# A first mixer fed with a turned copy of x, both first convolutions ahead of the query and key work, and output rows placed among scores and turns

## The chip, the cores and the metric

The kernel runs on one core of a Trainium2 chip. The metric is the time of one execution on the device in microseconds: the median of several runs. A core has TensorE (PE in the rows; weight loads are PEld), VectorE (DVE), ScalarE (ACT), GpSimd (POOL) and the sync engine (SP), each with a queue of its own that it works off in order, and 16 DMA engines. All data are float32.

## The reference

Two transformer blocks over 256 tokens of width 1024, with 16 meta tokens in front in the first. A block is a mixer and a mixture of experts (32 experts, two per token, and a shared one). The change touches the first mixer and the kernel's last lines. The first mixer, cut:

```
h = concat([meta, x]);  z = rms_norm(h, pre_mix_norm) @ w_in
c_q, c_kv, k_pe, gate_b, gate_c, x_in = split(z)          # 256, 128, 32, 3 x 512 columns
q  = (rms_norm(c_q, q_norm) @ w_uq)   -> 8 heads, 64 plain + 32 rope columns
kv = (rms_norm(c_kv, kv_norm) @ w_ukv) -> k_nope, v;  k_rope = rope(k_pe)
attn = causal softmax attention over meta and tokens
u = gate_c * x_in;  y[t] = sum_k conv_w[k] * u[t-2+k];  conv = gate_b * y
out = concat([rms_norm(attn), rms_norm(conv)]) @ w_out
h = h + rms_norm(out);  h = h + rms_norm(moe(rms_norm(h)))
```

The second block is alike, with differential attention and retention as its mixer, and a final norm.

## The kernel before

**Products.** Every large product of the mixers is done as three: each operand is split into a high half and the rest (a low half), and `mm3` (L319 to L321) adds high by high, high by low and low by high into one PSUM bank. Of a weight the high half is a ScalarE copy (L294) and the low half a subtraction (L295) on VectorE for a chunk's first half and on GpSimd for its second. `prepare` makes one such part; `part` hands out the oldest prepared one and prepares the next. The first mixer has 20 parts: 12 for the three convolution inputs (four each) and 8 for the output weights, of which the conv branch's four come first.

**Weights.** Chunks of 1 MB stream through 26 slots. `plan` gives their order; the sync engine issues the next load when a slot is free (`ahead`, `fits`). An engine's work is in the order in which the program writes it; nothing reorders it later.

**The first mixer's sequence.** x and the meta tokens are loaded row by row of tokens and turned on TensorE: 24 transposes (L432, L434). ScalarE and VectorE take the eight turned pieces out as high and low halves times the norm's gain. W_a (the columns for c_q, c_kv and k_pe) is split into four parts (`split_wa`), and z comes out in three banks (eight steps of k). Squares of x give the row scales, positions give angles, and ScalarE's Sin gives the rope factors. Then: `conv(0)` (gate_c, four quarters m of 24 matmuls), transposes of c, query product (L606) and key/value products, `conv(1)` (x_in, taps in `gated`), `turn_q` (16 transposes, L649), `conv(2)` (gate_b, ends in `conv_done`, which leaves the conv branch's mixed parts `mc` in halves). Scores (L679, mask L681) follow: four banks of two heads for the first 128 queries, eight banks of one head for the second; VectorE takes the maximum (L682), ScalarE the exponential (L685), then four multiplications by the reciprocal sums (L692), two on VectorE and two on GpSimd. `w_out` adds one part i of the four of a branch into a bank for a half t of the queries and a half e of the columns. Parts 0 and 1 of `mc` come first (24 matmuls), then all 24 turns of the probabilities (`turn_p`, L727), the branch's row scale (`feat_rstd`, `turn_m`), parts 2 and 3 for t = 0, `attend(0)`, those for t = 1, and `attend(1)`. `attend` (L742, L747) leaves the attention branch's halves `ma`, whose rows with the last four weight parts follow, then the residual, the router and MoE 1, whose first expert product is L1501.

**The tail.** The last norm of the output multiplies by its gain in quarters as MoE 2 ends (`after`, L1184), sums squares, and scales by the root (L1202, L1204) before the stores.

Of the kernel before, what the change touches and what calls it, by code (L numbers as in the profile page):

```python
# [75 lines left out]
def layout(i):  # L76
# [5 lines left out]
    o["pos"] = np.ascontiguousarray(f["positions"].reshape(2, 128).T)  # L82
    kt = lambda w: w.reshape(-1, 128, w.shape[1]).transpose(1, 0, 2)
    w = g("w_in")
# [46 lines left out]
    for n, grp in enumerate(CONST_GROUPS):  # L131
        o[f"c{n}"] = np.concatenate([cs[k] for k in grp], 1)
    o["c2"] = np.concatenate([o["c2"], o.pop("lam")], 1)
# [18 lines left out]
def plan():  # L152
# [14 lines left out]
    yield from (("wa", 0), ("wa", 1), ("wc", 0), ("wc", 1), ("wuq",), ("wukv",), *[("wc", j) for j in range(2, 6)])  # L167
# [16 lines left out]
class Builder:  # L184
# [73 lines left out]
    def source(self, key):  # L258
        if key[0] == "pmg":
            r = self.a["pmg"]  # L260
            return [bass.AP(tensor=r.tensor, offset=r.offset, ap=[[0, 128], [1, D]]), self.a["wr"][0]]
        if key == ("dn2", 15, 3):
# [82 lines left out]
    def setup(self):  # L345
        nc, P, a = self.nc, self.P, self.a
        self.h = P.tile([128, 2, D], F32, name="h")
        nc.sync.dma_start(self.h[:, 0], a["x"][0:128])
        self.meta = self.slot([NM, D], "meta")
        nc.sync.dma_start(self.meta, a["meta"])  # L350
        nc.sync.dma_start(self.h[:, 1], a["x"][128:256])
        self.k = self.const(P.tile([128, self.coff[0][1]], F32, name="const0"), 0, nc.scalar)
        self.small = P.tile([128, self.sn], F32, name="small")
        nc.scalar.dma_start(self.small, a["small"])
        self.pos = P.tile([128, 2], I32, name="pos")
        nc.scalar.dma_start(self.pos, a["pos"])
        self.s = {k: self.small[:, o:o + w] for k, (o, w) in self.soff.items()}
        self.bef = P.tile([128, 128], BF, name="bef")
        self.onesb = P.tile([128, 128], BF, name="onesb")
# [4 lines left out]
        nc.gpsimd.memset(self.mhalf, -0.5)  # L364

    def late_setup(self, before):
# [3 lines left out]
        nc.gpsimd.memset(self.onesb, 1.0)  # L370
# [29 lines left out]
    def mixer1(self):  # L400
# [5 lines left out]
        k1 = self.const(gen, 1, nc.scalar)  # L406
# [17 lines left out]
        piece = lambda i: xp[i // 7][:, i % 7] if i < 14 else self.GS[:, (i - 14) * 258:(i - 14) * 258 + 258]  # L424
        xh, xl = [piece(2 * k) for k in range(8)], [piece(2 * k + 1) for k in range(8)]
        xm = cT[:, 0:128].rearrange("p (k t) -> p k t", t=NM)
        self.ahead()
        self.late_setup(k1["before"])
        ps = [bank() for _ in range(8)]
        for t in range(2):  # L430
            for k in range(8):
                PE.transpose(ps[k][:, NM + t * 128:NM + t * 128 + 128], h[:, t, k * 128:k * 128 + 128], id_)  # L432
                if t == 0:
                    PE.transpose(ps[k][:, 0:NM], meta[:, k * 128:k * 128 + 128], id_[:NM, :NM])  # L434
        wat, wa = [], []

        def split_wa(j):
            raw = self.chunk("wa", j)
            wat.append(raw)
            for e in range(2):  # L440
                w = self.slot([128, 2, 1024], "wa", F32R)
                x = raw[:, e * 832:e * 832 + 832]
                A.activation(w[:, 0, :832], x, AF.Copy)
                (V, nc.gpsimd)[e].tensor_tensor(w[:, 1, :832], x, w[:, 0, :832].bitcast(F32), op=OP.subtract)
                wa.append(w)

        for k in range(8):
            gain, p = s["pmn"][:, k:k + 1], ps.pop(0)
            A.activation(xh[k], p[:, NM - 2:TA], AF.Copy, scale=gain)
            V.scalar_tensor_tensor(xl[k], p[:, NM - 2:TA], gain, xh[k].bitcast(F32), op0=OP.mult, op1=OP.subtract)  # L450
            V.tensor_scalar(xm[:, k], p[:, 0:NM], gain, None, op0=OP.mult)
            if k == 1:
                split_wa(0)
        split_wa(1)
        za = [bank() for _ in range(3)]
        for k in range(8):
# [6 lines left out]
            if k % 4 == 3:  # L463
                self.free(wat[k // 4], *wa[k // 2 - 1:k // 2 + 1])
        idb, tri = sub([128, 64]).bitcast(BF), sub([128, 64]).bitcast(BF)
# [6 lines left out]
        for j, x in ((0, h[:, 0]), (2, meta)):  # L472
            n = x.shape[0]
            for e in range(2):
                A.activation(bank()[:n], x[:, e * 512:e * 512 + 512], AF.Square,
                             accum_out=ss[:n, 3 * e + j:3 * e + j + 1])
        ang = sub([128, 2, 3, 16])
# [21 lines left out]
        for e in range(2):  # L499
            sl = slice(e * 512, e * 512 + 512)  # L500
            V.scalar_tensor_tensor(junk, h[:, 1, sl], 1.0, h[:, 1, sl], op0=OP.mult, op1=OP.mult,
                                   accum_out=ss[:, 3 * e + 1:3 * e + 2])
        V.tensor_tensor(ss[:, 0:3], ss[:, 0:3], ss[:, 3:6], op=OP.add)
        rx = self.rms(ss[:, 0:3], 3, D)
# [6 lines left out]
        p = bank()  # L511
        self.spread(p[:, 0:NM], rx[:NM, 2:3], NM)
        for t in range(2):
            self.spread(p[:, NM + t * 128:NM + t * 128 + 128], rx[:, t:t + 1])
        rxx = sub([128, 258])
        A.activation(rxx, p[:, NM - 2:TA], AF.Square)
# [42 lines left out]
        def conv(i, done):  # L559
            for m in range(4):  # L560
# [213 lines left out]
        for t in range(2):  # L774
# [6 lines left out]
            if t == 0:  # L781
                self.prepare()
# [955 lines left out]
```

## Time and profile before

| | before |
|---|---|
| median of three runs | 936.5 us (935.39 to 937.39) |
| profiled execution | 936.15 us |
| its span, first to last instruction | 934.4 us |
| mean granted TensorE clock | 0.956 of full |
| TensorE / VectorE / ScalarE / GpSimd busy | 845.6 / 389.6 / 227.0 / 118.8 us |
| moved by DMA | 340.88 MB |
| first convolution begins, third ends | 30.24 us, 81.76 us |
| second attend ends | 116.00 us |
| MoE 1's first expert product begins | 143.51 us |

Shares are of the span. Busy time includes waits for data inside an instruction, so a TensorE that is 91% busy is not one at its peak. The trace lets one look at a stretch, an engine or a line alone; the rows used are shown below.

### The profile page before, as it was taken

Reading aid. Unit: us, or ns where it says so; the run is one execution under the profiler, and the core shown is the slowest. Engines: PE = TensorE matmul, PEld = TensorE weight load, DVE = VectorE, ACT = ScalarE, POOL = GpSimd, SP = SyncE. Lnnn points to the kernel's source line nnn. Section 1 sums busy time; section 2 is a strip of 40 time slices with the busy share of each in tenths; the row PEclk is TensorE's granted clock in tenths of the full one; section 3 lists DMA queues with packets and bytes.
Section 4 is the critical chain, followed back from the end, with each engine's and each line's share of the span. In section 5 each row is a group of like instructions: output and inputs, shape, how many; then the busy total and the mean of one; then the engine's idle time right before and its main releaser. Section 6 shows DMA issues by size and latency. Waiting matters only on the chain. (4 is left out here: it accounts for less than half of the span.)

```text
span 934.4 us, 12196 instructions
## 1 busy us (share of the span) xinstructions
PE 845.6 (91%) x4789; PEld 469.0 (50%) x4789; DVE 389.6 (42%) x789; ACT 227.0 (24%) x473; POOL 118.8 (13%) x83
## 2 busy tenths in 40 slices
PE   7999999997967858997989999999999998799995
PEld 4788775553431316996874443434343432334332
DVE  4867672443322368576451224232333331133313
ACT  5346522211110135372312102111111110011113
POOL 3322520000000047634300000000000000000002
PEclk9999999998977897997999999999999999899998
DMA  9925498999999999553799999999999999999994
GB/s 363 415 95 221 160 385 354 420 419 418 420 420 420 421 421 421 219 178 138 271 364 368 421 415 391 421 421 422 420 422 420 421 422 421 416 422 421 421 420 169
DMA packets 48631, 340.88 MB, mean 365 GB/s; under 512 B 5536, under 2 KB 6176, under 8 KB 8112
## 3 DMA queue, kind: packets, MB, share of 16 engines
q1 hardware_dynamic: 47408, 338.55, 88.7%
q10 hardware_dynamic: 1152, 1.41, 0.5%
q8 instruction: 42, 0.69, 0.3%
q14 instruction: 29, 0.24, 0.1%
HBM read 338.88 MB, written 1.05 MB: 364 GB/s over the span
## 5 line engine op out<-in xcount | busy, mean ns | idle before, releaser
L1501 PE MATMUL bank<-chunk,xe 128*64 128x512 f32 (+1 forms) x1536 | 293.6, 618 | 27.8 <-DMA chunk<-in_gu_dram 15.0
L1501 PEld LDWEIGHTS bank<-chunk,xe 128*64 128x64 f32 (+1 forms) x1536 | 88.0, 130 | 218.2 <-issue 197.6
L1574 PE MATMUL bank<-chunk,hids 128*64 128x512 f32 (+1 forms) x736 | 143.3, 618 | 19.9 <-DMA chunk<-in_dn_dram 19.4
L1574 PEld LDWEIGHTS bank<-chunk,hids 128*64 128x64 f32 (+1 forms) x736 | 40.8, 128 | 117.4 <-issue 75.5
L295 POOL TENSOR_TENSOR w<-chunk,w 128x1024 fp32r<-128x1024 f32 x28 | 69.7, 2497 | 78.2 <-ACT w L294 65.4
L1578 DVE SCALAR_TENSOR_TENSOR ys<-bank,wc,ys 128x512 fp32r<-128x512 f32 x46 | 34.5, 750 | 98.1 <-ACT ys L1577 98.1
L1507 DVE TENSOR_TENSOR hids<-bank,hids 128x512 f32<-128x512 f32 x12 | 8.3, 692 | 158.0 <-PE bank L1501 158.0
L1577 ACT ACTIVATE ys<-bank,wc 128x512 fp32r<-128x512 f32 x46 | 31.6, 687 | 143.8 <-PE bank L1574 135.3
L1184 POOL TENSOR_TENSOR out<-acc,rows 128x256 f32<-128x256 f32 x6 | 4.3, 730 | 439.2 <-DVE acc L1692 439.1
L294 ACT ACTIVATE w<-chunk 128x1024 fp32r<-128x1024 f32 x52 | 52.4, 1053 | 22.0 <-DVE w L295 11.5
L1596 DVE TENSOR_TENSOR acc<-acc,bank 128x512 f32<-128x512 f32 x84 | 52.1, 680 | 13.3 <-PE bank L1589 13.3
L1512 DVE SCALAR_TENSOR_TENSOR hids<-bank,misc,hids 128x256 f32<-128x256 f32 (+1 forms) x12 | 6.9, 572 | 113.9 <-ACT hids L1511 70.7
L1506 ACT ACTIVATE hids<-bank 128x512 f32<-128x512 f32 x12 | 7.2, 597 | 181.6 <-PE bank L1501 181.6
L1347 PEld LDWEIGHTS bank<-GS,h 128*128 128x128 f32 x384 | 45.5, 197 | 10.7 <-issue 5.1
L1589 PE MATMUL bank<-ys,GS 128*128 128x512 f32 x184 | 49.5, 408 | 1.3 <-ACT ys L1577 1.3
L1347 PE MATMUL bank<-GS,h 128*128 128x128 f32 x384 | 47.8, 284 | 1.6 <-DVE GS L1355 1.6
L1511 ACT ACTIVATE hids<-bank,misc 128x256 f32<-128x256 f32 (+1 forms) x12 | 6.5, 546 | 136.0 <-PE bank L1501 136.0
L295 DVE TENSOR_TENSOR w<-chunk,w 128x1024 fp32r<-128x1024 f32 x24 | 35.7, 1494 | 8.8 <-ACT w L294 8.7
L948 PE MATMUL bank<-w,xT 128*128 128x512 f32 x144 | 37.8, 422 | 0.6 <-DVE xT L902 0.6
L1589 PEld LDWEIGHTS bank<-ys,GS 128*128 128x128 f32 x184 | 32.5, 188 | 10.9 <-ACT ys L1577 2.2
L948 PEld LDWEIGHTS bank<-w,xT 128*128 128x128 f32 x144 | 29.0, 205 | 7.8 <-DVE xT L902 1.7
L860 POOL TENSOR_TENSOR xn<-h,rows 128x1024 f32<-128x1024 f32 x2 | 4.7, 2388 | 188.3 <-DVE misc L1557 188.3
(401 smaller groups left out, 1187.1 us busy)
## 6 DMA issues: line engine op xcount, KB each, us to landing
chunk<-in_gu_dram SPq DMA_DIRECT2D x192, 1024.0 KB, 19.8
chunk<-in_dn_dram SPq DMA_DIRECT2D x95, 1024.0 KB, 19.8
chunk<-in_wi_dram SPq DMA_DIRECT2D x12, 1024.0 KB, 19.5
chunk<-in_wo_dram SPq DMA_DIRECT2D x8, 1024.0 KB, 15.9
chunk<-in_wc_dram SPq DMA_DIRECT2D x6, 1024.0 KB, 13.6
chunk<-in_sgu_dram SPq DMA_DIRECT2D x2, 1024.0 KB, 9.5
chunk<-in_wa_dram SPq DMA_DIRECT2D x2, 832.0 KB, 6.9
h<-in_x_dram SPq DMA_DIRECT2D x2, 512.0 KB, 5.4
```

Source lines behind the costliest of these rows:

```text
L294: self.nc.scalar.activation(w[:, 0], raw, AF.Copy)
L295: (eng or (self.nc.vector, self.nc.gpsimd)[e]).tensor_tensor(w[:, 1], raw, w[:, 0].bitcast(F32), op=OP.subtract)
L948: PE.matmul(p[t], xT[x][:, 2 * i + k, t * 128:t * 128 + 128], w[:, s, k * 512:k * 512 + 512], start=i + x + s + k == 0, stop=i + x == 4 an ...
L1347: b.nc.tensor.matmul(self.pb[k // 4][:, k % 4 * 128:k % 4 * 128 + 128], b.h[:, t, k * 128:k * 128 + 128], G[:, t].bitcast(F32), start=t == ...
L1501: PE.matmul(g[i][e * C:e * C + C], xe[:, k, e * C:e * C + C], c[:, e, i * 512:i * 512 + 512], start=k == 0, stop=k == 7)
L1506: A.activation(hid, g[0], AF.Silu)
L1507: V.tensor_tensor(hid, g[1], hid, op=OP.mult)
L1574: PE.matmul(y[e * C:e * C + C], hT[:, o:o + C], c[:, f, e], start=q + f == 0, stop=fpc * q + f == FC - 1)
L1577: A.activation(ys[:, 0, i], y, AF.Copy, scale=wc)
L1578: V.scalar_tensor_tensor(ys[:, 1, i], y, wc, ys[:, 0, i].bitcast(F32), op0=OP.mult, op1=OP.subtract)
L1589: PE.matmul(ps[t], S[:, t * 128:t * 128 + 128], ys[:, i, e], start=i == 0, stop=i == 1)
L1596: V.tensor_tensor(o, b.h[:, t, sl] if new else o, p, op=OP.add)
```

## The change

- **Start.** A turned copy of x (1 MB) and of the meta tokens is read from DRAM, and the transposes are gone. The constants, the small vectors and the positions arrive in one transfer; ScalarE does an early copy. TensorE does 60 small bfloat16 products (`warm`) ahead of z. x itself is loaded whole behind W_a. The splits of W_a stand between the pieces k. The squares and the row scale come ahead of the angles.
- **Order of the convolutions.** `conv(0)` and `conv(1)` both stand ahead of the query and key work, and the plan loads all four of their chunks first. `turn_q` goes between the second and third quarter of `conv(2)`.
- **Output rows.** The eight rows of parts 0 and 1 follow one by one the eight scores of the second queries; part 2 follows them, and part 3 stands between the turns. The two attends follow each other. The last two of the attention branch's weight parts, of which one was made by the second call of `part` and one between the attends, are made by `part` behind the second attend.
- **Tail.** The last quarter's gain is multiplied together with the root, and the scaling is 512 columns on ScalarE and twice 256 on VectorE.

The core of the diff:

```diff
-        ps = [bank() for _ in range(8)]
-        for t in range(2):
-            for k in range(8):
-                PE.transpose(ps[k][:, NM + t * 128:NM + t * 128 + 128], h[:, t, k * 128:k * 128 + 128], id_)
...
+        xt = self.slot([128, 8, T], "xt")
+        for j in range(2):
+            nc.sync.dma_start(xt[:, 4 * j:4 * j + 4].rearrange("p k t -> p (k t)"), self.a["xt"][j])
+            raw[j] = self.chunk("wa", j)
+        nc.sync.dma_start(h, self.a["x"].rearrange("(t p) d -> p t d", p=128))
...
         for k in range(8):
-            gain, p = s["pmn"][:, k:k + 1], ps.pop(0)
-            A.activation(xh[k], p[:, NM - 2:TA], AF.Copy, scale=gain)
+            gain = s["pmn"][:, k:k + 1]
+            A.activation(xh[k][:, 2:258], xt[:, k], AF.Copy, scale=gain)
...
+            if k in (1, 3, 4):
+                split_wa(k // 4, k // 3 % 2 if k < 4 else 0)
...
-        conv(0, lambda m, p: V.tensor_tensor(u[:, m], p, rxx, op=OP.mult))
+        conv(0, lambda m, p: V.tensor_tensor(u[:, m], p, rxx, op=OP.mult),
+             between={0: spread_rx})
...
+        conv(1, gated)
...
-        conv(2, conv_done)
+        conv(2, conv_done, {2: turn_q})
...
+        pc = {(t, e): bank() for t in range(2) for e in range(2)}
+        w = [self.part(0) for _ in range(2)]
+        rows = [(t, e, i) for i in range(2) for t in range(2) for e in range(2)]
...
+                if t:
+                    r = rows[h0]
+                    w_out(pc, mc, *r, w[r[2]])
...
+        turn_p(0, 0)
+        turn_p(0, 1)
         for e in range(2):
-            turn_p(0, e)
-            turn_p(1, e)
...
+            w_out(pc, mc, 0, e, 3, w[1])
+        turn_p(1, 0)
+        for e in range(2):
+            w_out(pc, mc, 1, e, 3, w[1])
+        turn_p(1, 1)
...
-        w = [self.part(), self.part()]
-        for t in range(2):
-            for i in range(2):
-                for e in range(2):
-                    w_out(pc, mc, t, e, 2 + i, w[i])
+        for t in range(2):
             for e in range(2):
                 A.activation(mix[:, t, e * 512:e * 512 + 512], pc[t, e], AF.Copy, scale=rc[:, t:t + 1])
             attend(t)
-            if t == 0:
-                self.prepare()
         self.phase(0, 7)
         w = [self.part() for _ in range(4)]
...
             for t in range(2):
+                A.activation(o[:, t, 0:512], o[:, t, 0:512], AF.Copy, scale=r[:, t:t + 1])
+                V.scalar_tensor_tensor(o[:, t, 768:D], moe.acc[:, t, 768:D], r[:, t:t + 1], made["rows"][:, 768:D],
+                                       op0=OP.mult, op1=OP.mult)
+                V.tensor_scalar(o[:, t, 512:768], o[:, t, 512:768], r[:, t:t + 1], None, op0=OP.mult)
```

Three places show the new order. The first is TensorE at the turns of the probabilities, before (w are weight parts, mc the conv branch's mixed parts, P the probabilities, pT and cT turned copies):

```order
L319 MATMUL bank<-w,mc 128x512
L320 MATMUL bank<-w,mc 128x512
L321 MATMUL bank<-w,mc 128x512
L727 MATMUL bank<-const_74,P 128x128 x24
L708 MATMUL bank<-ones,chunk 128x1 x2
L735 MATMUL bank<-const_74,cT 128x128 x2
L319 MATMUL bank<-w,mc 128x512
L320 MATMUL bank<-w,mc 128x512
```
and in the change:

```order
L324 MATMUL bank<-w,mc 128x512
L325 MATMUL bank<-w,mc 128x512
L326 MATMUL bank<-w,mc 128x512
L760 MATMUL bank<-const_72,P 128x128 x8
L324 MATMUL bank<-w,mc 128x512
L325 MATMUL bank<-w,mc 128x512
L326 MATMUL bank<-w,mc 128x512
L324 MATMUL bank<-w,mc 128x512
L325 MATMUL bank<-w,mc 128x512
L326 MATMUL bank<-w,mc 128x512
L760 MATMUL bank<-const_72,P 128x128 x8
```
The 24 turns stood in one piece behind the rows of parts 0 and 1; now rows of part 3 (the six behind the first eight turns, and six more later) stand between them.

The second place is ScalarE from the last weight copies of the softmax's end to the residual, before (L294 is a weight's high half, L313 and L749 an attend's copy and square):

```order
L294 ACTIVATE w<-chunk 128x1024 x2
L779 ACTIVATE mix<-bank,rs 128x512 x2
L313 ACTIVATE ma<-cT 128x4x128
L749 ACTIVATE vy<-bank 128x4x128
L294 ACTIVATE w<-chunk 128x1024
L779 ACTIVATE mix<-bank,rs 128x512 x2
L313 ACTIVATE ma<-cT 128x4x128
L749 ACTIVATE vy<-bank 128x4x128
L375 ACTIVATE bank,nss<-mix 128x512 x2
```
and in the change (L299, L318 and L782 are the same lines):

```order
L810 ACTIVATE mix<-bank,rs 128x512 x2
L318 ACTIVATE ma<-cT 128x4x128
L782 ACTIVATE vy<-bank 128x4x128
L810 ACTIVATE mix<-bank,rs 128x512 x2
L318 ACTIVATE ma<-cT 128x4x128
L782 ACTIVATE vy<-bank 128x4x128
L299 ACTIVATE w<-chunk 128x1024 x2
L385 ACTIVATE bank,nss<-mix 128x512 x2
```
The weight copy between the attends is gone, and two stand behind the second attend's square.

The third is GpSimd around the softmax's multiplications, before (L692 is the multiplication, L295 a low half, L331 a root):

```order
L295 TENSOR_TENSOR w<-chunk,w 128x1024 x6
L692 TENSOR_TENSOR P<-P,gen_87 128x576
L692 TENSOR_TENSOR P<-P,gen_87 128x1088
L295 TENSOR_TENSOR w<-chunk,w 128x1024
L331 TENSOR_TENSOR rs<-ms,mhalf 128x2
L295 TENSOR_TENSOR w<-chunk,w 128x1024 x2
L331 TENSOR_TENSOR rs<-ms,mhalf 128x2
```
and in the change (L730, L300, L336):

```order
L300 TENSOR_TENSOR w<-chunk,w 128x1024 x6
L730 TENSOR_TENSOR P<-P,gen_143 128x576
L730 TENSOR_TENSOR P<-P,gen_143 128x1088
L300 TENSOR_TENSOR w<-chunk,w 128x1024 x2
L336 TENSOR_TENSOR rs<-ms,mhalf 128x2
L300 TENSOR_TENSOR w<-chunk,w 128x1024
L336 TENSOR_TENSOR rs<-ms,mhalf 128x2
```
Behind the multiplications two low halves follow each other where one stood, and one instead of two comes between the roots.

## Rows read from the trace of the kernel before

**Rows 1.** Table of stretches: start:end, length, busy us (instructions) per engine, clock, DMA share, GB/s.

```profile
46.00:70.00 24.00, 24.00 (x141) 19.41 (x140) 14.91 (x24) 9.91 (x17) 4.72 (x2) 0.93 0.29 103
...
150.00:350.00 200.00, 163.36 (x1116) 73.58 (x1108) 71.13 (x140) 35.98 (x82) 12.01 (x8) 0.91 1.01 420
...
450.00:900.00 450.00, 433.17 (x2179) 199.66 (x2179) 140.45 (x297) 68.15 (x130) 5.60 (x5) 0.99 0.99 407
```

**Rows 2.** Timeline of the sync engine's queue: start, length, line, operation.

```profile
144.63 6.33 SPq L255 DMA_DIRECT2D chunk<-in_gu_dram  x8
```

**Rows 3.** Timeline of TensorE, the first expert product of MoE 1.

```profile
143.51 1.92 PE L1501 MATMUL bank<-chunk,xe 128*32 128x512 f32 x16
```

**Rows 4.** Waits of TensorE up to 150 us: line waited for, total, times, longest.

```profile
PE bank L606 <- DVE cT L588: 2.1, 1, 2.1
...
PE bank L679 <- ACT P L685: 1.7, 1, 1.7
```

**Rows 5.** Timeline of TensorE from the scores to the second attend and behind it.

```profile
81.76 0.41 PE L679 MATMUL bank<-kT,qT 96*128 96x144 f32 x2
...
88.76 0.73 PE L679 MATMUL bank<-kT,qT 96*128 96x272 f32 x2 [1.74 <-ACT P L685]
...
90.94 1.24 PE L679 MATMUL bank<-kT,qT 96*128 96x272 f32 x2
...
94.61 0.39 PE L319 MATMUL bank<-w,mc 128*128 128x512 f32 x1
...
98.69 2.78 PE L727 MATMUL bank<-const,P 128*128 128x128 f32 x24
...
116.00 0.50 PE L319 MATMUL bank<-w,ma 128*128 128x512 f32 x1
...
118.88 0.75 PE L708 MATMUL bank<-ones,chunk 128*128 128x1 f32 x4
```

**Rows 6.** Timeline of ScalarE at the start: Sin, and weight copies behind it.

```profile
25.56 0.28 ACT L506 ACTIVATE gen<-gen 128x96 f32<-128x96 f32 x1 [3.16 <-DVE gen L498]
...
25.75 1.99 ACT L294 ACTIVATE w<-chunk 128x1024 fp32r<-128x1024 f32 x2
```

**Rows 7.** Timeline of VectorE: three small operations, and a weight's low half.

```profile
34.31 4.70 DVE L535 TENSOR_TENSOR rs<-rs 128x2 f32<-128x2 f32 x3 [0.82 <-POOL rs L331]
...
41.52 1.22 DVE L295 TENSOR_TENSOR w<-chunk,w 128x1024 fp32r<-128x1024 f32 x1
```

**Rows 8.** Timeline of TensorE: first convolution's first matmul, and what follows its last.

```profile
30.24 0.37 PE L319 MATMUL bank<-xp,w 128*128 128x258 f32 x1
...
41.96 0.23 PE L576 MATMUL bank<-const,cn 16*128 16x16 f32 x1
```

**Rows 9.** Timeline of GpSimd beside rows 7.

```profile
34.24 4.75 POOL L295 TENSOR_TENSOR w<-chunk,w 128x1024 fp32r<-128x1024 f32 x2
```

**Rows 10.** Timeline of VectorE: last maximum, a low half, last reduction of squares.

```profile
92.32 0.44 DVE L682 TENSOR_REDUCE gen<-bank 128x1 f32<-128x272 f32 x1 [0.85 <-PE bank L681]
...
97.18 2.40 DVE L295 TENSOR_TENSOR w<-chunk,w 128x1024 fp32r<-128x1024 f32 x1
...
118.12 1.06 DVE L703 TENSOR_REDUCE chunk<-vy 128x128 f32<-128x512 f32 x1
```

**Rows 11.** Timeline of GpSimd: softmax multiplication, two low halves.

```profile
95.38 1.16 POOL L692 TENSOR_TENSOR P<-P,gen 128x576 f32<-128x576 f32 x1 [12.06 <-DVE gen L691]
...
98.46 3.35 POOL L295 TENSOR_TENSOR w<-chunk,w 128x1024 fp32r<-128x1024 f32 x1
...
112.17 2.36 POOL L295 TENSOR_TENSOR w<-chunk,w 128x1024 fp32r<-128x1024 f32 x1 [6.40 <-ACT w L294]
```

**Rows 12.** Timeline of ScalarE: a weight copy between the attends, last square.

```profile
111.04 1.05 ACT L294 ACTIVATE w<-chunk 128x1024 fp32r<-128x1024 f32 x1
...
117.39 0.58 ACT L749 ACTIVATE vy<-bank 128x512 f32<-128x512 f32 x1
```

**Rows 13.** Timeline of VectorE in the tail.

```profile
926.79 0.75 DVE L1184 TENSOR_TENSOR out<-acc,rows 128x256 f32<-128x256 f32 x2
...
927.46 0.15 DVE L1195 TENSOR_REDUCE nr<-nss 128x1 f32<-128x4 f32 x1
```

More of the change, by code (lines that the diff above doesn't have):

```diff
@@ L165, in experts @@
         yield from ((f"dn{n}", units - 1, j) for j in range(4))
-    yield from (("wa", 0), ("wa", 1), ("wc", 0), ("wc", 1), ("wuq",), ("wukv",), *[("wc", j) for j in range(2, 6)])
+    yield from (("wa", 0), ("wa", 1), *[("wc", j) for j in range(4)], ("wuq",), ("wukv",), ("wc", 4), ("wc", 5))
     yield from (("wo", 2), ("wo", 3), ("wo", 0), ("wo", 1), ("pmg",), ("sgu", 0), ("sgu", 1))
@@ L261, in source @@
             return [bass.AP(tensor=r.tensor, offset=r.offset, ap=[[0, 128], [1, D]]), self.a["wr"][0]]
+        if key[0] == "wa":
+            return [self.a["wa"][key[1]][:, e * 832:e * 832 + 832] for e in range(2)]
         if key == ("dn2", 15, 3):
@@ L364, in setup, with warm @@
         nc.gpsimd.memset(self.mhalf, -0.5)
+        nc.scalar.activation(self.ones[:, 1:2], self.mhalf[:, 0:1], AF.Copy)
+        self.warm(60)
+    def warm(self, n):
+        p = self.bank()
+        for _ in range(n):
+            self.nc.tensor.matmul(p[:, 0:128], self.onesb, self.onesb, start=True, stop=True)
     def late_setup(self, before):
@@ L557, in mixer1, with conv @@
              sin[:, :, None, :].to_broadcast([128, 3, 2, 16]), 3)
-        def conv(i, done):
+        def conv(i, done, then=(), between=()):
             for m in range(4):
+                if m in then:
+                    then[m]()
                 w = self.part()
@@ L752, in mixer1 @@
         self.phase(0, 5)
-        pc = {(t, e): bank() for t in range(2) for e in range(2)}
-        for i in range(2):
-            w = self.part(0)
-            for t in range(2):
-                for e in range(2):
-                    w_out(pc, mc, t, e, i, w)
-            self.free(w)
+        w = [self.part(0), self.part(0)]
+        for t in range(2):
+            for e in range(2):
+                w_out(pc, mc, t, e, 2, w[0])
         for t in range(2):
@@ L763, in mixer1 @@
         self.phase(0, 6)
+        turn_p(0, 0)
+        turn_p(0, 1)
         for e in range(2):
-            turn_p(0, e)
-            turn_p(1, e)
-        self.free(*PP)
+            w_out(pc, mc, 0, e, 3, w[1])
+        turn_p(1, 0)
+        for e in range(2):
+            w_out(pc, mc, 1, e, 3, w[1])
+        turn_p(1, 1)
+        self.free(*PP, *w, mc)
         rc = feat_rstd(rx[:, 0:2])
@@ L1183, in after @@
                                           accum_out=ss[:, t, q:q + 1])
[L1184 to L1187 removed]
+                if q < 3:
+                    self.nc.gpsimd.tensor_tensor(made["out"][:, t, sl], moe.acc[:, t, sl], made["rows"][:, sl],
+                                                 op=OP.mult)
+        self.link = moe, made, ss, r
         return after
```

154 lines of the change are left out of this document (75 added, 79 removed).

## The prediction

> **What bounds the kernel now.** I read the table of stretches first. From 150 us on, except in the second mixer, the DMA engines are never free: 420 GB/s and a busy share of 1.01 from 150 to 350, 407 GB/s and 0.99 from 450 to 900 [rows 1]. The first mixer lies ahead of those stretches, so the next question is what lets that stream begin. The sync engine's queue shows it: a burst of eight expert chunks is issued from 144.63 [rows 2], right after TensorE begins the first expert product at 143.51 [rows 3]. The slots that the burst fills are freed by that product. Behind it the stream runs at its own pace, so **a microsecond that the first mixer ends earlier or later moves the end of the kernel by a microsecond**. From 46 to 70 DMA stands at 0.29: bandwidth is not what the first mixer waits for. The list of waits says that TensorE hardly waits there either, 2.1 us for the normalised c_q (L606) and 1.7 us for a bank among the scores (L679) [rows 4]. So TensorE's sequence, with its clock, is the path up to 143.51, and every new wait on it is paid in full.
>
> Half clock follows both waits. From 90.94 the pair of score matmuls takes 1.24 us where the one at 88.76 took 0.73, and the output rows come back to their pitch at 94.61 [rows 5]: 3.67 us go to work that takes 2.1 at the pitches on either side, so 1.6 us are lost. After the wait of 2.1 the table shows 24 us at a mean clock of 0.93 [rows 1], which is 1.7 us lost. I use **1.6 us for one spell at half clock**.
>
> The sum is made against the profiled execution's 936.15 us; the median of the runs shown, 936.5, lies 0.35 above, well inside the 0.2% (1.9 us) that a measurement of this kernel can tell from no change.
>
> **The change, part by part.** Below, S is the end of the third convolution and start of the scores, L the end of the last score, T the end of the second attend.
>
> *Start, -1.4.* The 24 transposes leave TensorE, and the 60 warm-up products stand where it has nothing to do, since it waits for the turned copy. But the first convolution doesn't wait for TensorE alone. Its second weight half is copied by ScalarE right behind the Sin, at 25.75 now [rows 6], and the Sin stays behind the angles on VectorE, with the squares of x now ahead of them. I estimate Sin at 25, the copy until 26.2 and the low half, 1.22 us [rows 7], until 27.5. Three quarters of a convolution, at 2.9 each from 30.24 to 41.96 for four [rows 8], then end at 36.3, 5.6 us before the old 41.96. Most of that goes back: the second convolution now follows at once, and its first weights have their low half on VectorE, behind c's normalisation, the rope and the first u. Those stand behind GpSimd's low halves: three small VectorE operations took 4.70 us [rows 7] while GpSimd made two of them in 4.75 us [rows 9], and now three stand in a row. By these rows the low half comes at about 39.9: 3.6 us. Half a spell at half clock or a slightly longer wait on c_q takes 0.6. S is 1.4 earlier. Bounds: nothing given back, -5.6; all given back, 0. I stand nearer the second because every step of the giving back has a row. The extra megabyte at the start moves later transfers by about 2.5 us at 420 GB/s [rows 1]; the cover is the weights' lead, and without it the copy above starts that much later, which the bound of 0 holds.
>
> Those rows show small VectorE operations standing for as long as GpSimd's subtractions run. The Trainium skill, SBUF — State Buffer, section "SBUF: two separate sides", says that VectorE and GpSimd share one port pair as an exclusive lock, and whichever began second blocks entirely. It speaks against this change, which puts more of GpSimd's long subtractions in a row. The trace agrees: 4.70 beside 4.75. Were it not so, the start would keep about 4 us more; that case is the third rival.
>
> *Scores, -0.3.* Output rows of the first two mixed parts move between the scores of the second half of the queries. The wait for a bank remains: the first exponentials free the banks as late as before (7.0 us after S, at 88.76 [rows 5]). From there six scores at 0.57 and six rows of three matmuls at 0.23 [rows 5] take 7.6, with 0.4 for the exponentials that free the following banks, and a half-clock spell 1.6 as now: rows done 16.6 after S, where now it is 16.9, from 81.76 to 98.69 [rows 5]. But **the last score, L, comes only 0.7 us before the last row**, no longer six.
>
> *First new wait, +4.7.* What was cover is gone. Before, the last maximum is taken at 92.32 [rows 10], GpSimd starts its two softmax multiplications at 95.38 and the low half of the fourth weight part at 98.46, 3.35 us long [rows 11]: it is there at 101.81, 9.5 after the last score, while TensorE has eight output rows, 24 turns and four more rows to do. In the changed sequence TensorE does after L one row (0.7), four rows of the third part (2.8), four turns, then waits for GpSimd's first multiplication (L + 4.2) and does four more turns; at L + 4.7 it wants that low half, which still stands third in GpSimd's queue: L + 9.4. Queued behind the waiting matmul are all remaining turns and both attends, and nothing on TensorE can go round it. Bounds: 3.7 if the low half takes the 2.36 of row 112.17 [rows 11] instead of 3.35, 4.9 by the rows as they stand. VectorE has again a low half beside it, as at 97.18 [rows 10], so I take the upper part.
>
> *Between, 0.* The work from 98.69 to 116.00 [rows 5] is the same matmuls in another order. The turned q and the spread of the row scales, moved inside convolutions, last as long there as where they stood.
>
> *Second new wait, +4.2.* The last two parts of the output weights are now prepared after the second attend; one of them was done between the attends on ScalarE at 111.04 (1.05 us) [rows 12] and GpSimd at 112.17 (2.36) [rows 11]. Now both copies stand in ScalarE's queue behind the last square, which ends at 117.97 [rows 12], 2.0 after T = 116.00 [rows 5]: copies done at T + 3.0 and T + 4.0, the third part's low half on VectorE behind the reduction that ends at 119.18 [rows 10], so T + 4.4, the fourth's on GpSimd at T + 6.4. TensorE needs them from T + 1.4. The group of twelve matmuls that ended at T + 2.9 (118.88 [rows 5]) ends at T + 7.1. Bounds: 3.6 if ScalarE's copies overlap the square, 4.5 if GpSimd's runs beside a VectorE operation.
>
> *Clock, +2.4.* Both known waits of 1.7 to 2.1 us were followed by a spell at half clock. The first new one is longer than either and of one piece: 1.6. The second comes in three pieces with matmuls between: half, 0.8. Bounds 0 and 3.2 for both.
>
> *End, -0.3.* The last quarter's multiplication (two of 0.75 together on VectorE at 926.79) no longer stands ahead of the sums at 927.46 [rows 13]; the squares on ScalarE limit the gain to about 0.3. Bounds 0 and -0.7.
>
> Sum: -1.4 - 0.3 + 4.7 + 4.2 + 2.4 - 0.3 = +9.3, so **945.5 us**.
>
> **The rivals.** *Both splits in time (faster).* If the fourth weight part's low half were ready within 4.7 us after the last score, and the last two weight parts before T + 1.4, neither wait would exist: -1.4 - 0.3 - 0.3 gives 934.1, and without the spell among the scores, which the rows between them could prevent, 932.5. It decides at GpSimd: three of its instructions, 3.1 + 3.35 us after reciprocals that need the last maximum, must take less than 4.7 in all. For it: the multiplications would be shorter with VectorE idle. Against: each stands on TensorE's path by its own queue, and even 2.36 for the third leaves 8.4. Chance 0.18.
>
> *Only one wait bites.* Second alone: 936.15 - 2.0 + 4.2 + 0.8 = 939.2; first alone: 936.15 - 2.0 + 4.7 + 1.6 = 940.5. For it: the two waits are independent, and either needs only one GpSimd run to end some 4 us sooner than its row says. Chance 0.13.
>
> *The start keeps its gain.* If the lock on the low halves doesn't hold c back, S comes up to 5.6 earlier; with both waits that is 945.5 - 4.2 = 941.3. For it: TensorE has 6.5 us less to do there. Against: rows 7 and 9. Chance 0.08.
>
> *The warm-up doesn't do what it says:* the products end, TensorE stands for the copies of x, and z runs slowly as now. TensorE is not what the first convolution's second quarter waits for, so this changes no sum and is inside the first term.
>
> **How the numbers follow.** The forecast, both waits with at least one spell, has 0.61. Its own range is the bounds: below, no spells (-2.4), the shorter low half (-1.0) and half the start's giving back (-2.1), not all at once, 940.5; above, the full clock price (+0.8), S unmoved (+1.4), waits at their upper ends (+0.5) and a little for later transfers, 949.5. The single-wait cases reach to 938. I range 937.5 to 949.5, which leaves out the first rival. Faster by over 0.2%: most of the first rival, 0.16. Within 0.2%: its rest, where a small wait eats the gain, and the lower end of the single-wait case, 0.07. Slower: 0.77.
>
> **What would show it.** Right: TensorE's list of waits gains a row for the low half of a weight part made by GpSimd, some 4 to 5 us, in the middle of the turns, and rows for the last two parts, 3 to 4 us in all, after the second attend; the first expert product begins near 153, and the burst of eight expert chunks a microsecond later. Wrong: these rows are missing or under a microsecond, the second convolution runs on from the first without a wait, or that product begins later without the end moving, which would break the first step.

## The result, and the profile after

The change makes the kernel slower: 949.89 us median (949.03 to 952.37), against 936.18 (935.39 to 937.39) for the kernel before in the same comparison. The ratio is 1.015, with a 95% interval of 1.0128 to 1.0172. The forecast was 945.5 with a range of 937.5 to 949.5: the direction and the two waits were right, the size was 4.4 us short, and the time lies 0.4 us outside the range.

The profiled execution took 949.79 us, its span is 948.0, 13.6 more than before. TensorE's waits up to the first expert product, in the view whose columns are line waited for, total, times and longest, are these:

```profile
PE bank L325 <- POOL w L300: 5.6, 2, 4.3
PE bank L326 <- DVE w L300: 4.3, 2, 3.5
PE bank L645 <- DVE cT L627: 2.1, 1, 2.1
PE bank L324 <- ACT w L299: 1.9, 2, 1.3
...
PE bank L714 <- ACT P L720: 1.3, 1, 1.3
...
PE bank L325 <- DVE w L300: 0.9, 1, 0.9
```

Where [rows 4] have two waits, there are now also four rows for weight parts (`w`), made by GpSimd, VectorE and ScalarE; some of their waits stand in the first two convolutions, the others in the turns and behind the second attend. The timeline of TensorE answers to [rows 3, 5]:

```profile
42.07 0.39 PE L326 MATMUL bank<-xp,w 128*128 128x258 f32 x1 [3.52 <-DVE w L300]
...
83.22 0.41 PE L714 MATMUL bank<-kT,qT 96*128 96x144 f32 x2
...
90.06 0.72 PE L714 MATMUL bank<-kT,qT 96*128 96x272 f32 x2 [1.25 <-ACT P L720]
...
97.28 0.22 PE L716 MATMUL bank<-gen 128*128 128x128 bf16 x1
...
98.08 0.39 PE L324 MATMUL bank<-w,mc 128*128 128x512 f32 x1
...
102.21 0.48 PE L324 MATMUL bank<-w,mc 128*128 128x512 f32 x1
107.03 0.79 PE L325 MATMUL bank<-w,mc 128*128 128x512 f32 x1 [4.34 <-POOL w L300]
...
122.67 0.50 PE L324 MATMUL bank<-w,ma 128*128 128x512 f32 x1
...
125.64 0.49 PE L324 MATMUL bank<-w,ma 128*128 128x512 f32 x1 [1.31 <-ACT w L299]
127.03 0.50 PE L325 MATMUL bank<-w,ma 128*128 128x512 f32 x1 [0.89 <-DVE w L300]
...
129.25 0.79 PE L325 MATMUL bank<-w,ma 128*128 128x512 f32 x1 [1.26 <-POOL w L300]
...
130.26 0.85 PE L746 MATMUL bank<-ones,chunk 128*128 128x1 f32 x4
...
156.68 1.91 PE L1530 MATMUL bank<-chunk,xe 128*32 128x512 f32 x14
```

The scores begin at 83.22 instead of 81.76; the eight rows are done at 98.08, 14.9 later instead of 16.9; the wait of 4.34 stands in the turns; the second attend ends at 122.67 instead of 116.00; behind it the group of twelve matmuls takes 7.6 instead of 2.9; and the first expert product begins at 156.68 instead of 143.51. From there to the end it is 791.3 us against 790.9. So 13.2 of the 13.6 us arise ahead of that product, and the step "a microsecond there is a microsecond at the end" held. The other engines, in the same timeline:

```profile
25.62 0.28 ACT L523 ACTIVATE gen<-gen 128x96 f32<-128x96 f32 x1 [2.29 <-DVE gen L521]
...
32.83 7.07 POOL L300 TENSOR_TENSOR w<-chunk,w 128x1024 fp32r<-128x1024 f32 x3
...
32.90 4.70 DVE L554 TENSOR_TENSOR rs<-rs 128x2 f32<-128x2 f32 x3 [0.82 <-POOL rs L336]
...
40.80 1.22 DVE L300 TENSOR_TENSOR w<-chunk,w 128x1024 fp32r<-128x1024 f32 x1
...
100.59 3.11 POOL L730 TENSOR_TENSOR P<-P,gen 128x576 f32<-128x576 f32 x2 [15.98 <-DVE gen L729]
103.66 5.65 POOL L300 TENSOR_TENSOR w<-chunk,w 128x1024 fp32r<-128x1024 f32 x2
...
124.54 1.99 ACT L299 ACTIVATE w<-chunk 128x1024 fp32r<-128x1024 f32 x2
...
126.61 2.58 POOL L300 TENSOR_TENSOR w<-chunk,w 128x1024 fp32r<-128x1024 f32 x1 [11.59 <-ACT w L299]
```

GpSimd's multiplications begin at 100.59, its low halves behind them at 103.66, and TensorE goes on at 107.03, 9.5 us after the last score's end at 97.50; both weight copies stand behind the second attend on ScalarE at 124.54. That is the queue of the forecast, to 0.1 us. The clock is what differs. Five stretches of half clock lie ahead of the first expert product (columns as in [rows 1]: the granted clock is the third value from the end, 0.50 is 1.2 of 2.4 GHz):

```profile
29.10:32.40 3.30, 3.30 (x18) 3.30 (x17) 1.00 (x8) 3.02 (x12) 0.71 (x1) 0.50 1.04 425
42.80:46.10 3.30, 3.30 (x18) 3.30 (x17) 1.35 (x2) 0.00 (x0) 0.00 (x0) 0.50 1.03 413
59.90:63.20 3.30, 3.30 (x6) 1.75 (x6) 1.57 (x2) 0.62 (x2) 0.00 (x0) 0.50 0.08 30
104.20:110.90 6.70, 3.87 (x14) 3.28 (x14) 1.18 (x2) 0.47 (x1) 5.11 (x2) 0.50 0.00 0
128.10:134.80 6.70, 5.55 (x15) 4.59 (x16) 0.91 (x2) 0.72 (x2) 2.83 (x3) 0.50 0.70 256
```

Before, the granted clock shows two spells of 3.4 us, one at the query product and one among the scores [rows 1, 5]. Each of the five follows a place where TensorE stood, or begins in one: 0.57 and 0.75 us in the first convolution, 3.52 in the second, 2.1 for c_q, and the two waits for weight parts. The granted clock reads 1.00 at the very start of both traces, but the pitch of the matmuls doesn't bear that out for the kernel before: its products for z, 416 columns each, follow each other at 0.35 us until about 19 us and at 0.19 afterwards, where the change has 0.19 from 9.2 us on.

### The profile page after: what moved, and what is told of

Same layout as the page of the kernel before. It is cut to its first block, busy times and chain, and to the rows that moved or that the text cites. A ratio compares the mean times of both kernels' runs of the same rounds, so it can differ in the third digit from the quotient of the medians.

```text
span 948.0 us, 12266 instructions
## 1 busy us (share of the span) xinstructions
PE 850.1 (90%) x4825; PEld 474.8 (50%) x4825; DVE 386.1 (41%) x786; ACT 228.4 (24%) x474; POOL 117.5 (12%) x83
## 5 line engine op out<-in xcount | busy, mean ns | idle before, releaser
L300 POOL TENSOR_TENSOR w<-chunk,w 128x1024 fp32r<-128x1024 f32 x28 | 69.7, 2500 | 89.3 <-ACT w L299 76.4
L299 ACT ACTIVATE w<-chunk 128x1024 fp32r<-128x1024 f32 x52 | 52.1, 1048 | 26.7 <-DVE w L300 11.5
L1625 DVE TENSOR_TENSOR acc<-acc,bank 128x512 f32<-128x512 f32 x84 | 52.1, 681 | 13.2 <-PE bank L1618 13.2
L300 DVE TENSOR_TENSOR w<-chunk,w 128x1024 fp32r<-128x1024 f32 x24 | 35.7, 1496 | 10.8 <-ACT w L299 10.8
L326 PE MATMUL bank<-xp,w 128*128 128x258 f32 x84 | 25.2, 300 | 4.3 <-DVE w L300 4.3
```

The source lines that it names most:

```text
L299: self.nc.scalar.activation(w[:, 0], raw, AF.Copy)
L300: (eng or (self.nc.vector, self.nc.gpsimd)[e]).tensor_tensor(w[:, 1], raw, w[:, 0].bitcast(F32), op=OP.subtract)
L326: PE.matmul(out, x[1], w[0], start=False, stop=stop)
L1625: V.tensor_tensor(o, b.h[:, t, sl] if new else o, p, op=OP.add)
```

## The experiments

Each was compared with the kernel before on its own chip. The medians of that kernel lie between 934.4 and 936.2 us from chip to chip, so where runs from different chips differ by less than 2 us, the ratios count and not the medians. From one trace of each, S is the start of the first score, T the second attend's end, E the start of the first expert product, in us:

| run | median us | ratio to before, 95% | S | S to T | T to E |
|---|---|---|---|---|---|
| before | 936.18 | 1 | 81.76 | 34.24 | 27.51 |
| the change | 949.89 | 1.015 [1.0128, 1.0172] | 83.22 | 39.45 | 34.01 |
| r1 second half alone | 949.80 | 1.0154 [1.0133, 1.0174] | 81.01 | 40.01 | 34.23 |
| r2 start alone | 935.44 | 0.9995 [0.9978, 1.0012] | 83.45 | 35.33 | 29.60 |
| r3 fourth part early | 947.58 | 1.0125 [1.0108, 1.0143] | 83.39 | 37.26 | 33.03 |
| r4 last parts early | 944.52 | 1.0085 [1.0066, 1.0104] | 83.20 | 43.05 | 27.93 |
| r5 both | 939.00 | 1.0033 [1.0014, 1.0052] | 82.83 | 37.65 | 28.80 |
| r6 both, rows between attends | 937.15 | 1.0015 [1.0001, 1.0030] | 83.16 | 34.13 | 27.74 |
| r7 start, old convolution order | 934.22 | 0.9986 [0.9976, 0.9995] | 81.04 | 34.36 | 27.51 |
| r8 start, wait filled | 936.75 | 1.0008 [0.9987, 1.0028] | 79.78 | 35.32 | 27.77 |
| r9 change, first wait filled | 948.16 | 1.0137 [1.0108, 1.0165] | 82.52 | 37.72 | 34.56 |
| r10 start, no warm-up | 938.00 | 1.0024 [1.0006, 1.0042] | 80.38 | 33.16 | 27.74 |
| r11 r7, waits filled | 933.99 | 0.9982 [0.9969, 0.9995] | 78.59 | 34.38 | 27.53 |
| r12 before, wait filled | 935.53 | 0.9994 [0.9979, 1.0008] | 79.49 | 35.48 | 27.51 |
| r13 change, start filled | 948.77 | 1.0146 [1.0117, 1.0175] | 80.06 | 43.06 | 33.62 |
| r14 change, all waits filled | 944.68 | 1.0112 [1.0070, 1.0155] | 78.94 | 41.99 | 31.55 |

**Which half: r1 and r2.** r1 takes the change from the scores to the second attend into the kernel before; r2 is the change with that stretch as before. The lines in brackets stand for the code of that stretch, which is the one of the diff above:

```diff
         self.phase(0, 4)
-(r1: the lines before; r2: the lines of the change)
+(r1: the lines of the change; r2: the lines before)
...
         self.phase(0, 7)
```

> The kernel before with the change's second half alone: from the scores to the second attend the changed sequence, all else (start, order of the convolutions, tail) as before. Theory A (the two waits for weight parts, each with a spell at half clock, are the loss): 936.2 - 2.1 (scores without a half-clock spell) + 7.3 (first wait and spell) + 6.5 (second) = 947.9 us. Rival B (the start's loss makes the later waits worse, or they arise only from it): under 943 us.

> The change with the sequence from the scores to the second attend put back as before; the new start, the order of the convolutions and the new tail stay. Theory A: the third convolution ends about 1.5 us later than before, the tail gives 0.2 back: 937.5 us (936.5 to 938.5). Rival B: 943 us or more, if the start carries the loss. Rival C (the forecast's first step held and only the trace's reading differs): 934.8 us.

r1 measures 949.8, theory A's 947.9 and 1.9 more: **the second half is the whole loss.** Its waits are the change's own:

```profile
PE bank L320 <- POOL w L295: 5.6, 2, 4.3
...
PE bank L319 <- ACT w L294: 1.3, 1, 1.3
...
PE bank L320 <- DVE w L295: 0.9, 1, 0.9
```

r2 can't be told from the kernel before. Its ten times spread from 932.8 to 940.3 and the profiled one is the longest, so its column T to E (a half-clock spell lies in it) is not typical. Rival B of both falls. Theory A of r2 fails too: 935.4 lies below its 936.5 to 938.5, so the 1.5 us by which the scores begin later in the trace don't show in the times. Rival C, that the start gains as forecast, is inside r2's interval and so not excluded.

**Undoing one wait: r3 and r4.** r3 makes the fourth part between the scores of the first and the second queries, r4 the last two ahead of the first attend:

```diff
+            if t == 0:
+                self.prepare()
```
```diff
+            if t == 0:
+                self.prepare(2)
             attend(t)
```

> The change with the fourth output-weight part prepared between the scores of the first and of the second queries, so that its low half is ahead of the softmax multiplications in GpSimd's queue. Theory A: the wait of 4.3 us in the turns and the half-clock spell behind it go, 949.9 - 4.7 - 1.8 = 943.4 us. Rival B (the turns then wait for GpSimd's multiplications, which end 6 us after the last score): a wait of 1.5 to 3 us in the same place remains, 946 to 948 us.

> The change with the last two weight parts prepared ahead of the first attend instead of behind the second. Theory A: the group of twelve matmuls behind the second attend takes 2.9 us instead of 7.6 and the half-clock spell behind it goes, 949.9 - 4.7 - 1.7 = 943.5 us. Rival B (the copies delay the attends' own copies on ScalarE and the wait moves to them): 946 us or more.

In both the wait aimed at is gone from the list, yet r3 gives 2.3 us where 6.5 were expected, and r4 5.4 where 6.4 were. Rival B of r3 asked for a wait left in the turns; the only one there is 0.3 us for GpSimd's multiplication, so it falls too. What came instead is in the table of stretches of r3, over both attends:

```profile
109.20:120.70 11.50, 11.47 (x65) 7.56 (x65) 2.51 (x4) 3.34 (x6) 0.00 (x0) 0.57 0.47 192
```

They took 11.4 us instead of the 7.2 of the change. Of the 11.5 us TensorE is counted busy all but 0.03, and the clock stood at a mean of 0.57. r4's S to T grew by 3.6 in the same way. This was a new theory D: the attends, put back to back, lose the clock by themselves.

**Both undone, and rows between the attends: r5 and r6.** r5 has both edits. r6 adds, with the rest of r5:

```diff
-        for e in range(2):
-            w_out(pc, mc, 0, e, 3, w[1])
         turn_p(1, 0)
-        for e in range(2):
-            w_out(pc, mc, 1, e, 3, w[1])
         turn_p(1, 1)
...
         for t in range(2):
+            for e in range(2):
+                w_out(pc, mc, t, e, 3, w[1])
```

> The change with both edits of r3 and r4: fourth weight part prepared among the scores, the last two ahead of the first attend; no wait for a weight part is left in the second half. Theory A (waits and the half-clock spells behind them were all of the loss there): from the last score to the second attend's end 18.5 us, from there to the first expert product 27.9, in all 937 us. Theory D (the two attends, back to back, lose the clock by themselves once no wait stands ahead of them, as r3's attends took 11.4 us at half clock against 7.2): 22.9 us and 27.9, in all 941.5 us.

> r5 with the rows of the fourth part where the kernel before had them: those of the first queries ahead of the first attend, those of the second between the attends; scores with rows, and all else, as in r5. Theory D: the dense rows keep the clock through the attends, 4 us less than r5: 937 us. Theory A: rows moved, no time changed against r5 (within 1 us).

Attends in r5, with 2.8 us of the rows behind them, then in r6:

```profile
109.70:123.30 13.60, 13.60 (x65) 9.15 (x65) 5.57 (x7) 5.28 (x8) 2.44 (x1) 0.50 0.55 193
```
```profile
108.70:117.30 8.60, 8.60 (x71) 6.00 (x71) 4.42 (x5) 5.27 (x8) 2.44 (x1) 1.00 0.97 402
```

r5's trace went as theory D said. Its median, 939.0, lies between the two theories: five of its times are 935.8 to 937.5, five 940.5 to 942.5. That would fit a spell that comes in some executions, but only one was traced, and the mean granted clocks of the two groups overlap (0.949 to 0.952 and 0.943 to 0.955), so it isn't shown. r6 keeps the clock through the attends in its trace, and its median is 1.9 lower, less than the 4 expected, and the two intervals overlap, so the size is not settled. Without any wait for a weight part, r6 takes 34.13 from S to T where the kernel before takes 34.24: the rows among the scores save the spell there, and the softmax's tail, now 3.8 us later, takes it back in small waits (0.7 for GpSimd's multiplications, 0.6 and 0.8 for turned copies). In this trace the interleaving wins nothing.

**The start: r7, r8, r10.** r7 puts the second convolution and its chunks back behind the query and key work of r2; r8 adds small products ahead of the second convolution in r2; r10 drops those of the setup from r2. In this order:

```diff
-        conv(1, gated)
...
+        conv(1, gated)
         qT = self.slot([96, 8, T], "qT")
```
```diff
+        self.warm(60)
         conv(1, gated)
```
```diff
         nc.scalar.activation(self.ones[:, 1:2], self.mhalf[:, 0:1], AF.Copy)
-        self.warm(60)
```

> r2 (new start, old second half) with the second convolution and the load order of its chunks put back behind the query and key work; the turned copy stays. Theory: the wait of 3.5 us for the low half of its first weights and the half-clock spell behind it go, the third convolution ends 4 to 5 us earlier than in r2 and the kernel at 931 us. Rival (what the start gains is lost before the scores in any order): 934 us or more.

> r2 with 60 small bfloat16 products ahead of the second convolution, about as long as its wait of 3.5 us; the wait's end can't change, only what TensorE does until then. Theory (the spell at half clock behind the wait comes from TensorE standing still): the spell of 3.4 us goes, the third convolution ends 1.6 us earlier than in r2. Rival (the spell comes anyway): no change within 0.3 us.

> r2 (new start, old second half) without the 60 warm-up products. By the forecast's reading: z runs slower at first, by up to 6 us, but the first convolution's second quarter waits for ScalarE's copy behind the Sin anyway, so the third convolution ends where it did (83.4) and the time is r2's 935.4 within 0.5. Rival: a late z delays that chain too, 1 to 4 us more.

r7's 934.2 goes to its rival, which asked for 934 or more. The wait of 3.5 is gone and one of 3.7 stands for c_q, where it was 2.1 [rows 4]:

```profile
PE bank L643 <- DVE cT L625: 3.7, 1, 3.7
```

The first convolution begins 7.6 us earlier (22.65 instead of 30.24), the scores 0.7: in either order TensorE ends up waiting for VectorE's queue, in which c's normalisation stands. r8's trace shows the theory's effect and more, all three spells of the start gone, and a longer one among the scores:

```profile
20.00:46.00 26.00, 23.77 (x211) 21.60 (x209) 18.17 (x47) 13.00 (x28) 10.89 (x6) 1.00 1.02 417
46.00:70.00 24.00, 21.86 (x131) 17.35 (x130) 16.25 (x25) 10.24 (x18) 4.82 (x2) 1.00 0.27 104
86.70:93.50 6.80, 6.80 (x18) 4.63 (x19) 3.52 (x9) 6.80 (x30) 0.00 (x0) 0.50 0.88 372
```

The scores begin 3.7 earlier than in r2, the time is no lower. r10 is inconclusive: its trace (933.1 us, among its shortest) has the scores at 80.4, earlier than r2's, so a late z did not delay the chain there: without the warm-up the first convolution begins 2.8 us later (25.43 instead of 22.66), the two short waits in it are gone, and so are the spells of r2 at 29 and 42 us; but its median is 2.6 above r2's, on another chip, with intervals that overlap by 0.06%.

**Filling the waits: r9, r11 to r14.** TensorE doesn't stand in a wait if it does small products until the wait ends. r9 does so in the change's first wait; r11 in r7, in the first convolution and ahead of the query product; r12 there in the kernel before; r13 is the change with r8's edit; r14 has that, r9's, and products in the second wait. r9, r11, r12 and r14's own part:

```diff
         turn_p(0, 1)
+        self.warm(75)
```
```diff
-             between={0: spread_rx})
+             then={1: lambda: self.warm(24)}, between={0: spread_rx})
...
+        self.warm(62)
         wuq = self.chunk("wuq")
```
```diff
+        p = bank()
+        for _ in range(38):
+            PE.matmul(p[:, 0:128], self.onesb, self.onesb, start=True, stop=True)
         wuq = self.chunk("wuq")
```
```diff
             for i in range(4):
+                if e == 0 and i > 1:
+                    self.warm((0, 0, 42, 20)[i])
                 w_out(pa, ma, 0, e, i, w[i])
```

> The change itself with 75 small bfloat16 products (about 4.2 us at the 0.055 of a product in r8) ahead of the rows of the fourth part, so that TensorE works through the first wait; the wait's end can't change. Theory (the clock is a cost of its own beside the wait): the half-clock spell behind the wait goes and 1.8 us with it, 948.1 us. Rival D' (the attends, back to back, then take the spell): no change, 949.9.

> r7 (new start, old order of the convolutions, old second half) with 24 small products ahead of the first convolution's second quarter and 62 ahead of the query product, where r7's TensorE stands 1.3 and 3.7 us and runs at half clock for 3.4 and 6.8 us afterwards. Theory: both spells go, the scores begin 4 us earlier than in r7 (77 us), and the kernel takes 930.5 us. Rival (a spell comes later instead): 932.5 us or more.

> The kernel before with 38 small products ahead of the query product, where it waits 2.1 us for c_q. Theory: the half-clock spell at 46.6 goes, 1.6 us: 934.0 us against 935.5 on this chip. Rival (spells only move): no change within 0.5 us.

> The change with 60 small products ahead of the second convolution, as in r8. In r8's trace all three half-clock spells of the start went and the scores began 3.7 us earlier, but the time did not fall, since a spell of 6.8 us came among the scores. In the change the scores have rows between them. Theory (the forecast's error in the start is spells alone, and the dense rows keep the clock among the scores): 949.9 - 3.4 = 946.5 us. Rival (spells move here too): 949 us or more.

> The change with small products in all three places: 60 ahead of the second convolution, 75 in the first wait (as in r9), 42 and 20 in the pieces of the second wait. The waits keep their ends. Theory: without spells the change costs its waits less what the start and the scores gain, 949.9 - 3.4 - 1.8 - 1.8 = 942.9 us, and the forecast's error of 4.3 us is then in its clock terms. Rival (spells move to other places): 946 us or more.

r9's median is the theory's number, 948.16 for 948.1, but part of that is luck: on its chip the kernel before is 1.4 us faster too, and by the ratios (1.0137 against 1.015) the gain is 1.2 us, with intervals that overlap. The trace carries it: the stretch that was at half clock is at full, S to T is 1.7 shorter, and the attends, back to back as they are, keep the full clock too:

```profile
104.20:110.90 6.70, 6.57 (x62) 5.66 (x59) 1.53 (x3) 0.74 (x2) 4.48 (x2) 1.00 0.14 23
113.00:120.30 7.30, 7.26 (x65) 4.92 (x65) 2.53 (x4) 3.35 (x6) 0.00 (x0) 1.00 0.72 299
```

r13 goes to its rival: the spells moved to the attends (10.0 us at 0.50). r12's interval holds its theory (a ratio of 0.998) and its rival, so its time decides nothing; in its trace the spell at the query product is gone, and the one among the scores lasts twice as long:

```profile
86.70:93.50 6.80, 6.80 (x18) 4.60 (x19) 3.61 (x9) 6.80 (x30) 0.00 (x0) 0.50 0.11 46
```

r14's median, 944.7, falls between theory and rival; its ratio, 1.0112, would be 946.7 for the change's chip and falls to the rival, and its interval holds both. In its trace, with all waits for weight parts behind the scores filled, the attends are at half clock:

```profile
109.70:119.90 10.20, 10.20 (x55) 6.40 (x53) 2.34 (x3) 3.02 (x6) 0.00 (x0) 0.50 0.48 199
```

From the first wait to T, r9 and r14 run the same instructions with the same small waits (0.32 and 0.9 us ahead of the attends). At full clock the attends take 7.2 us there, at half clock 11.5. So putting them back to back doesn't by itself decide for the slow clock.

r11 beats both kernels, the one before by 0.18% (0.05 to 0.31%), but it misses the 930.5 of its theory: its trace has the scores 2.5 earlier than r7's, one spell ahead of the fillers at 9.6 and one behind them at 88.1. r7 without fillers stands at 0.14% (0.05 to 0.24%), so the fillers' share can't be told from nothing. Neither uses the new second half.

## Why the prediction was wrong in size

The mechanism was forecast rightly: two new waits, at the forecast places and by the forecast queues, each with half clock. What failed are two terms of the sum, "Start, -1.4" and "Clock, +2.4". In the trace they are +1.5 and about +4.2; "Scores, -0.3" came out 1.8 better and hid part of it.

The medians share out the 4.4 us otherwise than the one trace. r1 has all terms of the second half (scores, both waits, clock): forecast +11.0, measured +13.9. r2 has the start and the tail: forecast -1.7, measured -0.5, with an interval of -2.1 to +1.1. So in time most of the shortfall is in the second half, and it isn't shown that the start lost anything.

**Right.** The 1:1 path to the end (13.2 of 13.6). The first wait: forecast 4.7, in the trace 4.34 for the low half and 0.40 for the multiplication ahead of it. r3 takes it away by the edit that the cause asks for. The second wait: the right place and queue; the twelve matmuls end 4.7 later, with the last two of them at half clock, and in r14, where no half clock lies there, 4.3 (120.93 to 128.09), for a forecast of 4.2. r4 takes it away. The tail: from the last accumulation's start to the last store's issue 4.24 us before, 3.93 now (939.90 to 943.83), the forecast's 0.3. The lines are before, then now:

```profile
926.12 0.75 DVE L1692 TENSOR_TENSOR acc<-acc,bank 128x256 f32<-128x256 f32 x2 [0.71 <-PE bank L1689]
...
930.36 0.35 ACTq L1205 DMA_DIRECT2D out_dram<-out  x1
```
```profile
939.90 0.75 DVE L1721 TENSOR_TENSOR acc<-acc,bank 128x256 f32<-128x256 f32 x2 [0.71 <-PE bank L1718]
...
940.89 0.16 DVE L1224 TENSOR_REDUCE nr<-nss 128x1 f32<-128x4 f32 x1 [0.24 <-ACT bank L1210]
...
943.83 0.35 ACTq L1233 DMA_DIRECT2D out_dram<-out  x1
```

**Wrong: "Start, -1.4".** The trace gives +1.5, 2.9 more. The chain was read in the right order, but it came later than estimated: Sin at 25.62, no earlier than the 25.56 of [rows 6] (estimate 25), although TensorE began the first convolution 7.6 us earlier; the three VectorE operations at 32.90, 1.4 before those of [rows 7], and again 4.70 us long beside GpSimd's row of low halves, of which there were three; the second convolution's low half at 42.0 where I had 39.9. The size failed on two things. One is this chain: r8's trace, with no spell at all in the start, has the scores at 79.78, where the forecast without its spells (the old one's 1.6 and the 0.6 for a new one) would have 78.2, so it came out 1.6 late. The other is the clock: the start holds three spells where I allowed for the old one and half of a new one. Two of them cost something, 3.4 us against r8 where I had 2.2; the one at 29.1 stands ahead of the wait of 3.52, whose end VectorE sets. And the bound "all given back, 0" was no bound: a kernel that waits in more places can lose more than it won. In time, r2 says that the start is worth nothing that can be told from zero, so these 2.9 us are one trace's reading, and how much of them other executions have stays open.

**Wrong: "Clock, +2.4".** I priced the second spell at half because matmuls stand between its pieces. Both spells in the second half are 6.7 us long, twice those of [rows 1, 5], though part falls on standing time: T to E grew by 6.5; in r14, with the wait filled and no half clock there, by 4.0, so 2.5 of it is clock, not 0.8. For the first, rows done to T grew by 7.3, 4.7 of it wait; r9's trace puts 1.7 on the clock, where I had 1.6, and 0.9 stay unassigned.

**Wrong, the other way: "Scores, -0.3".** I left the spell among the scores in. It did not come, and the stretch gave 2.1. Summed over the trace: +1.5 - 2.1 + 7.3 + 6.5 + 0.4 = 13.6.

**Wrong: "Between, 0".** The same matmuls in another order were costed at nothing. Of the eight traces with the attends back to back, five (r3, r4, r5, r13, r14) have a spell at half clock of 10 us and more, 9 us and more of it over them; of the eight with rows between (before, r2, r6 to r8, r10 to r12) none has. In the change itself the attends ran at full clock (7.2 us), so the error is not in the sum; it shows in the attempts to undo the waits. That the rows between keep the clock is a reading that fits these traces, but it has a rival that no run tests: the same eight traces also have rows directly ahead of the first attend, where the others have the waits of 0.32 and 0.89 us with almost no work between. No run has rows in only one of the two places, and another filler between the attends was not tried.

The rivals of the prediction: "both splits in time" and "only one wait bites" didn't happen. r3 and r4 are the latter made by hand, at 947.6 and 944.5, well above the 939.2 and 940.5 worked out for it, for the reason just named. "The start keeps its gain" falls with r2 and r7. The Trainium skill's rule on the shared port pair (SBUF — State Buffer, section "SBUF: two separate sides") agrees with the trace once more: VectorE's three small two-input operations took 4.70 us beside 7.07 us of GpSimd's subtractions, and no run contradicts it. Two of the three lasted 2.35 us each, about as long as one subtraction (2.4). No run took the subtractions off GpSimd at that place, so what the lock alone costs was not measured.

Open stays when a spell comes in an execution. The same instructions have it or not (r9 and r14 in the attends; the short waits of the first convolution bring one in the change and none in r8 and r9), and medians move less than traces suggest.

## What to carry to other kernels

When instructions are moved, look at each in-order queue for what they used to hide: here a low half that had eight output rows, 24 turns and four rows as its cover was left with a third of it, and a part moved behind the second attend waited behind work that TensorE did not need yet. Where a wait is undone, check the clock of what follows before counting the gain, since a microsecond of wait removed can come back as half clock in what follows (r3 got 2.3 of 6.5 us); and cost a reordering of the same matmuls too. A first bound on a gain that is "given back" is not zero: count the places where the engine stands, not only the time.

## What the runs showed of the hardware

Filling a wait with small products kept the granted clock at 1.00 through the next stretch (r9), and from 20 to 70 us at the start (r8, r11). It didn't make the kernel as much faster as the trace promises where another stretch ran at 0.50 instead: in r12 the spell of 3.4 us at the query product was gone, the one among the scores lasted 6.8 us instead of 3.4, and the time was unchanged. TensorE that is busy all the time by the profile, with matmuls of 128 columns in the attends, ran at half clock through them in r5 (13.6 us with the rows behind them), and at full clock in r6; with the same instructions around them, at full clock in r9 and at half in r14.
